# Other costs and margins in the planner that orders a hybrid attention and state-space layer on one core

## The chip, the core and the metric

The kernel runs on one core of a Trainium2 chip. A core has five engines that run at the same time, each through its own list of instructions in order: TensorE (PE, matrix products; its weight loads are shown as PEld), VectorE (DVE), ScalarE (ACT), GpSimd (POOL) and SyncE (SP), which here only issues transfers. Sixteen DMA engines carry the transfers between memory and the core's SBUF. Products land in PSUM, from where DVE and ACT take them.

The metric is the time of one execution on the device in microseconds (us). The time before is the median of three runs; beside it stands one more execution that was profiled, and everything said of single instructions comes from that one.

## The reference

One layer of a streaming encoder is computed for two groups of requests that share the weights: a prompt of 1024 tokens and eight samples of 16 tokens, 1152 tokens in all.

```
h     = rms_norm(x, norm_g) * (1 + scale) + shift          # scale, shift, gate from silu(c) @ w_ada
q, k, v, z_att, z_ssd, xbc, dt_raw, gates = split(h @ w_in)
q, k  = rms_norm per head
att   = (softmax(q k^T / 8 + bias, masked to a band of 9 chunks of 64) v * silu(z_att)) @ w_att_proj
xbc   = silu(depthwise causal conv of width 4)             # -> x, B, C of the state-space branch
y     = chunked scan with decay exp(cumsum(dt * a)) over x, B, C  + d_skip * x
ssd   = rms_norm(y * silu(z_ssd), in 4 groups) @ w_ssd_proj
out   = x + gate * ((sigmoid(g_att) * att + sigmoid(g_ssd) * ssd) @ w_out)
```

The width of the model is 1024; there are 16 attention heads of 64 and 32 state-space heads of 64 with a state of 128. The samples attend to 512 cached rows and start from given states. The last keys, values, convolution rows and states are outputs too.

## The kernel before

**Tiling.** Tokens lie along the free axis in three groups of 384. Each large product is done in f16 with the weights and the operand split into a high and a low part: high times high, high times low, low times high, three matmuls of 128x128 against 384 columns for each block of 128 of the inner dimension (lines 689, 690 and 692 in `dense`, 742 to 744 in `dense_tok`, where the tokens are the stationary side). One tile of a result takes 8 such threes. It goes into a PSUM tile of the tag "d", of which there are three places; smaller products use the tag "g" (three places) and the tag "s" (one place of two banks).

**Stages.** First the modulation and the norm (until about 80 us of the profiled span), in an order that is fixed by hand. Then eight attention units of two heads each (to about 680 us), 16 pairs of state-space heads (to about 1380 us), and the three output projections with their merge gates. Within the attention stage a unit's queries and keys are normalised on POOL (`rsqrt_small`, lines 567 to 573, a power and two Newton steps; then the scaling at line 1220), transposed on PE (line 1240, and 1256 for the samples), copied out by DVE (line 1244), multiplied into scores on PE (line 1395; 1450 and 1453 for the samples), and turned into weights by DVE and ACT. The weights are transposed by a transfer that SP issues (line 1330; line 1472 for the samples, whose result DVE then puts in order at line 1474), and PE weighs the values with them (line 1348; 1483 for the samples). In the state-space stage the transfer at line 1759 does the like.

**Weights.** SP loads raw weight blocks (line 589) into three places. ACT and DVE make the high and low parts (lines 607 and 608); ACT also takes a sum of squares of each (line 599).

**The order.** The program is first written down by generators that take turns by a rough clock. Then the class `Order` makes the order in which each engine gets its instructions. It groups instructions into units (three matmuls of a dense product, or a run of small matmuls, are one unit), numbers them as they were written, finds what each must wait for, and plays the program through with a cost for each unit: `cost` gives how long it holds its engine and when its result is there. At each step the engine that can go on first gets a unit. Among the units of that engine that can start at that time, those whose inputs have been there for a margin ("sure" ones) go first, and among these the one written first; if none is sure, the first written of those that can start:

```
can = [u for u in ready[e] if u["now"] <= t]
sure = [u for u in can if u["safe"] <= t]
u = min(sure or can, key=lambda u: u["i"])
```

The margin is `SAFE` by the waiting engine, and `SAFE_DMA` where the input comes by a transfer. Units that open a PSUM tile must also find a place of its tag free. `apply` then ties each engine to the order found. The chip does not see the costs: they only decide which instruction stands before which, and an engine whose next instruction isn't ready waits, whatever stands behind it. Instructions marked with `late` keep the order in which they were written among those of their engine; almost everything until 80 us is so marked.

The transfers are planned in eight lanes for each issuing queue, used in turn; a transfer waits until the one before it in its lane has landed.

Of the kernel before, what the change touches and what calls it, by code (L numbers as in the profile page):

```python
# [14 lines left out]
ALU = mybir.AluOpType  # L15
# [19 lines left out]
AHEAD = 2  # L35
# [27 lines left out]
SP = 2.0 ** 12  # L63
# [75 lines left out]
class Order:  # L139


    SLOTS = {"d": 3, "g": 3, "s": 1}
    SAFE = {"PE": 500.0, "DVE": 300.0, "Activation": 300.0, "Pool": 0.0, "SP": 300.0}
    SAFE_DMA = 1500.0

    def __init__(self, tc, instructions, pinned, cuts):
        self.tc = tc
        self.list = [x for x in instructions if x.opcode != "TilePoolBoundary"]
        self.pinned, self.cuts = pinned, cuts

# [38 lines left out]
    def cost(self, x):  # L189

        e, op = self.engine(x), x.opcode
        outs = [a for a in x.outs if hasattr(a, "bass_ap")]
        ins = [a for a in x.ins if hasattr(a, "bass_ap")]
        p, n, dt = self.shape(outs[0])
        m = max([n] + [self.shape(a)[1] for a in ins[:1]])
        if e == "PE":
            rows, cols = x.tile_size
            moving = self.shape(ins[0])
            rate = 0.4245 * (4 if moving[2] == "float32" else 1)
            t = max(moving[1] * rate, 52.0 if rate < 1 else 105.0) * rows * cols / 16384  # L200
            return t, t + 170
        if op == "DMACopy":
            if e == "Pool":
                return 560.0, 4500.0
            return 380.0, 2600.0 + p * n * 4 / 300.0 if n * p > 4096 else 2600.0
        if op.startswith("DmaTranspose"):
            return 1350.0 if m < 2000 else 3200.0, 3200.0 + 1.0 * m
        if e == "Activation":
            t = 205 + 0.83 * m
            return t - 100 + 93 * (len(outs) > 1), t + 95 * (len(outs) > 1)  # L210
        if e == "DVE":
            if op == "TensorCopy":
                t = 165 + 0.57 * m
            elif op == "TensorReduce":
                t = 145 + 1.05 * m
            elif op == "TensorScalarPtr" and len([a for a in ins if self.shape(a)[1] > 1]) < 2:
                t = 215 + 0.52 * m
            elif op == "Reciprocal":
                t = 240 + m
            else:  # L220
                t = (210 if dt == "float16" else 180) + 1.04 * m
            return t - 80, t + 80 * (op == "ISA")
        if op == "Memset":
            return 200.0, 210.0
        t = 200 + 1.75 * m
        return t, t + 10

    def build(self):

        units, self.of, last = [], {}, None  # L230
        for x in self.list:
            e = self.engine(x)
# [8 lines left out]
            u = {"eng": e, "ins": [x], "i": len(units), "pred": {}, "succ": [], "key": None}  # L241
# [9 lines left out]
        for x in self.list:  # L251
            u = self.of[x.name]
            e = u["eng"]
# [4 lines left out]
            for a, w in acc:  # L258
                t, name, r0, r1, c0, c1 = self.region(a)
# [23 lines left out]
        for u in units:  # L283
            costs = [self.cost(x) for x in u["ins"]]
            u["busy"] = sum(c for c, _ in costs)
            u["lat"] = u["busy"] - costs[-1][0] + costs[-1][1]
            u["dma"] = any("Dma" in x.opcode or "DMA" in x.opcode for x in u["ins"])
        self.tiles = tiles
        opener = {}
        for name, (tag, us) in tiles.items():  # L290
# [13 lines left out]
    def run(self):  # L304

        units = self.units
        left = {u["i"]: len(u["pred"]) for u in units}
        engines = ["PE", "DVE", "Activation", "Pool", "SP"]
        free = dict.fromkeys(engines, 0.0)
        ready = {e: [] for e in engines}  # L310
        start, finish = {}, {}
        slots = {t: [0.0] * n for t, n in self.SLOTS.items()}
        lanes = {"SP": [0.0] * 8, "Pool": [0.0] * 8}
        nlane = {"SP": 0, "Pool": 0}
        order = {e: [] for e in engines}
        key = [None]
        log = []

        def add(u):
            r = safe = 0.0  # L320
            for j, kind in u["pred"].items():
                v = units[j]
                if v["eng"] == u["eng"] and not v["dma"]:
                    t = finish[j] if kind == 2 and u["eng"] != "PE" else start[j]
                    m = 0.0
                else:
                    t = finish[j] + 60
                    m = self.SAFE_DMA if v["dma"] else self.SAFE[u["eng"]]
                r = max(r, t)
                safe = max(safe, t + m)  # L330
            u["r"], u["safe"] = r, safe
            ready[u["eng"]].append(u)

        for u in units:
            if not left[u["i"]]:
                add(u)
        n = 0
        while n < len(units):
            best = None
            for e in engines:  # L340
                lane = 0.0
                for u in ready[e]:
                    r = u["r"]
                    for name in u.get("opens", ()):
                        s = slots[self.tiles[name][0]]
                        need = sum(self.tiles[o][0] == self.tiles[name][0] for o in u["opens"])
                        r = max(r, sorted(s)[need - 1] if len(s) >= need else 1e18)
                    u["now"] = r
                c = [u["now"] for u in ready[e]]
                if not c or min(c) > 1e17:  # L350
                    continue
                t = max(free[e], min(c))
                if best is None or t < best[0]:
                    best = (t, e)
            assert best, ("no unit can go on", [(e, [(u["i"], u["ins"][0].name) for u in ready[e]][:4]) for e in engines])
            t, e = best
            can = [u for u in ready[e] if u["now"] <= t]
            sure = [u for u in can if u["safe"] <= t]
            u = min(sure or can, key=lambda u: u["i"])
            ready[e].remove(u)  # L360
            for name in u.get("opens", ()):
                s = slots[self.tiles[name][0]]
                s.remove(min(s))
            if u["dma"]:
                k = nlane[e] % 8
                nlane[e] += 1
                t = max(t, lanes[e][k])
                lanes[e][k] = t + u["lat"]
# [8 lines left out]
            start[u["i"]], finish[u["i"]] = t, t + u["lat"]  # L377
# [12 lines left out]
            n += 1  # L390
        self.order, self.log, self.end = order, log, max(finish.values())
        self.start, self.finish = start, finish

# [9 lines left out]
def trunk_kernel(ctx: ExitStack, tc: tile.TileContext, h, again):  # L403
    nc = tc.nc
# [82 lines left out]
    n = (HCOLS - E0 - 3 * 1184 - 1024) // 1184  # L487
# [55 lines left out]
    dma = nc.sync.dma_start  # L543

    store = nc.gpsimd.dma_start
    pinned, cuts = set(), set()
    pinning = [True]

    def late(x):
# [15 lines left out]
    def rsqrt_small(v):  # L565

        late(nc.gpsimd.memset(v[2], -0.5))
        nc.gpsimd.tensor_tensor(v[1], v[0], v[2], ALU.pow)  # L568
# [1512 lines left out]
    order = Order(tc, list(nc.cur_bb.bb.instructions), pinned, cuts)  # L2081
    order.build()
    order.run()
    order.apply()
# [1859 lines left out]
```

## Time and profile before

| what | before |
|---|---|
| median of 3 runs | 1812.56 us (1806.89 to 1813.68) |
| profiled execution | 1813.1 us |
| its span, first to last instruction | 1810.6 us |
| mean granted clock of TensorE | 0.988 |
| PE busy | 1753.5 us (97%) |
| DVE, ACT, POOL busy | 1230.5, 959.7 and 351.2 us |
| share of the transfer engines | 51.4% for SP's queue, 4.2% for POOL's |

The span is shorter than the time of the execution by 2.5 us, which lie before the first and after the last instruction that the profile shows. In the rows, "waited for" names the instruction that released the waiting one; "PEclk" is the share of its full clock that TensorE was granted; "DMA" is the mean busy share of the 16 transfer engines. A matmul's own time in a row is longer than what it adds to the stream, since the next one starts before it ends. A time beside a transfer in the chain of waits runs from its issue to its landing.

### The profile page before, as it was taken

The page shows a single profiled execution, that of the slowest core. Times are in us where ns is not written, and L with a number is a line of the kernel's source. Part 1 is how long each engine was busy: PE and PEld are TensorE (multiplying, and loading weights), DVE is VectorE, ACT ScalarE, POOL GpSimd, SP SyncE. Part 2 cuts the span into 40 slices and gives each one's busy share as a digit, 9 for nine tenths or more (in the row PEclk, how much of TensorE's full clock was granted, in tenths as well). Part 3 has the DMA queues.
Part 4 walks back from the last instruction along what each step waited for, and adds up shares of the span by engine and source line. Part 5 has one row for each costly group of instructions (what it writes and reads, how often), then busy time and mean ns, then how long its engine had stood idle before and what let it go on. Part 6 is the DMA issues. An engine that isn't in the chain of part 4 may idle for free.

```text
span 1810.6 us, 34950 instructions
## 1 busy us (share of the span) xinstructions
PE 1753.5 (97%) x13821; PEld 1104.9 (61%) x13821; DVE 1230.5 (68%) x2327; ACT 959.7 (53%) x1905; POOL 351.2 (19%) x624
## 2 busy tenths in 40 slices
PE   6999999899999999999999999999999999999998
PEld 3556556566555556666666766666666556666664
DVE  4557767777777867767777777677775436876732
ACT  6866455565565647545556556555562625332510
POOL 0124134133322201222212132213122200000000
PEclk8999999999999999999999999999999999999999
DMA  9229968979689695533454354434567734311321
GB/s 368 74 74 226 197 181 183 194 204 214 165 233 201 158 209 150 150 116 125 117 151 139 114 152 154 143 119 107 155 200 271 289 129 142 103 41 60 126 101 55
DMA packets 266565, 284.87 MB, mean 157 GB/s; under 512 B 199628, under 2 KB 200664, under 8 KB 266392
## 3 DMA queue, kind: packets, MB, share of 16 engines
q1 hardware_dynamic: 257432, 253.90, 51.4%
q0 software_dynamic: 8960, 28.65, 4.2%
q8 instruction: 110, 1.80, 0.4%
q14 instruction: 63, 0.52, 0.1%
HBM read 192.70 MB, written 43.66 MB: 131 GB/s over the span
## 4 chain that ended last, share of the span: by engine, by line
PE 80%; DMA 6%; ACT 5%; DVE 4%; POOL 3%; issue 2%; SPq 0%; DVEq 0%; ACTq 0%; POOLq 0%
PE d L689 17%; PE d L692 17%; PE d L690 17%; PE d L742 4%; PE d L744 4%; PE d L743 4%; PE g L1348 2%; DMA arena<-arena 2%; PE s L1835 2%; PE g L1807 1%; PE s L1395 1%; PE g L1855 1%; POOL arena L568 1%; PE g L1395 1%; PE g L1483 1%
## 5 line engine op out<-in xcount | busy, mean ns | idle before, releaser
L689 PE MATMUL d<-arena 128*128 128x384 f16 x2172 | 710.7, 327 | 5.3 <-DVE arena L1978 2.7
L690 PE MATMUL d<-arena 128*128 128x384 f16 x2172 | 709.7, 327 | 0.0
L692 PE MATMUL d<-arena 128*128 128x384 f16 x2172 | 709.7, 327 | 0.0
L692 PEld LDWEIGHTS <-arena 128*128 128x128 f16 x2280 | 223.3, 98 | 148.1 <-issue 1.0
L689 PEld LDWEIGHTS <-arena 128*128 128x128 f16 x2280 | 223.5, 98 | 146.9 <-issue 7.7
L690 PEld LDWEIGHTS <-arena 128*128 128x128 f16 x2280 | 223.4, 98 | 143.5 <-issue 6.7
L599 ACT ACTIVATE arena<-arena 128x1024 bf16<-128x1024 f32 (+3 forms) x169 | 181.6, 1075 | 157.1 <-DMA arena<-in_wall_dram 86.3
L608 DVE SCALAR_TENSOR_TENSOR arena<-arena 128x1024 f16<-128x1024 f32 (+1 forms) x117 | 147.7, 1264 | 77.4 <-ACT arena L607 77.0
L607 ACT ACTIVATE arena<-arena 128x1024 f16<-128x1024 f32 (+1 forms) x117 | 122.4, 1047 | 131.0 <-PE d L690 115.0
L742 PE MATMUL d<-arena 128*128 128x384 f16 (+1 forms) x568 | 187.5, 330 | 0.0
L744 PE MATMUL d<-arena 128*128 128x384 f16 (+1 forms) x568 | 187.1, 329 | 0.0
L743 PE MATMUL d<-arena 128*128 128x384 f16 (+1 forms) x568 | 187.0, 329 | 0.0
L1288 ACT ACTIVATE arena<-arena 128x640 f32<-128x640 f32 (+3 forms) x144 | 100.7, 701 | 69.3 <-DVE arena L1291 69.0
L1546 DVE SCALAR_TENSOR_TENSOR arena<-arena 128x1176 f32<-128x1176 f32 x72 | 106.3, 1476 | 6.7 <-issue 4.8
L1734 ACT ACTIVATE arena<-arena 128x128 f32<-128x128 f32 x288 | 89.6, 388 | 11.4 <-DMA arena<-acs_d 11.3
L1216 POOL TENSOR_SCALAR arena<-arena 128x16 f32<-128x16 f32 (+1 forms) x24 | 13.4, 558 | 385.0 <-DVE arena L1189 324.6
L1324 DVE SCALAR_TENSOR_TENSOR arena<-arena 128x640 f16<-128x640 f32 (+4 forms) x128 | 87.6, 720 | 0.1
L742 PEld LDWEIGHTS <-arena 128*128 128x128 f16 x576 | 56.3, 98 | 50.3 <-issue 17.4
L744 PEld LDWEIGHTS <-arena 128*128 128x128 f16 x576 | 56.5, 98 | 38.7 <-issue 0.7
L1183 ACT ACTIVATE arena<-d 128x256 f32<-128x256 f32 x71 | 26.8, 377 | 95.3 <-PE d L744 95.1
L743 PEld LDWEIGHTS <-arena 128*128 128x128 f16 x576 | 56.5, 98 | 32.5 <-issue 0.2
L568 POOL TENSOR_TENSOR arena<-arena 128x16 f32<-128x16 f32 (+2 forms) x28 | 70.2, 2507 | 2.3
(244 smaller groups left out, 2614.4 us busy)
## 6 DMA issues: line engine op xcount, KB each, us to landing
arena<-in_wall_dram SPq DMA_DIRECT2D x85, 512.0 KB, 3.9
arena<-acs_d SPq DMA_DIRECT2D x32, 576.0 KB, 5.8
arena<-in_kc_dram SPq DMA_DIRECT2D x64, 256.0 KB, 4.4
arena<-in_vc_dram SPq DMA_DIRECT2D x64, 256.0 KB, 4.0
arena<-in_wada_dram SPq DMA_DIRECT2D x24, 512.0 KB, 10.0
arena<-in_xT_dram SPq DMA_DIRECT2D x16, 576.0 KB, 5.0
arena<-eacs_d SPq DMA_DIRECT2D x32, 288.0 KB, 6.0
gate_d<-arena POOLq DMA_DIRECT2D x48, 192.0 KB, 4.4
```

Source lines behind the costliest of these rows:

```text
L599: keep(nc.scalar.activation(junk[:, :n], x, AF.Square, scale=scale * n ** -0.5, accum_out=sums[:, c:c + 1]))
L607: keep(nc.scalar.activation(hi, x, AF.Copy, scale=scale))
L608: keep(nc.vector.scalar_tensor_tensor(lo, x, scale, hi, ALU.mult, ALU.subtract))
L689: nc.tensor.matmul(ps, hi.r[:, wc], kh.r[:, tok], start=k == 0, stop=False)
L690: nc.tensor.matmul(ps, hi.r[:, wc], kl.r[:, tok], start=False, stop=False)
L692: nc.tensor.matmul(ps, lo.r[:, wc], kh.r[:, tok], start=False, stop=k == nk - 1)
L742: nc.tensor.matmul(ps, kh.r[:, tok], wh, start=k == 0, stop=False)
L743: nc.tensor.matmul(ps, kh.r[:, tok], wl, start=False, stop=False)
L744: nc.tensor.matmul(ps, kl.r[:, tok], wh, start=False, stop=k == KT - 1)
L1288: nc.scalar.activation(p, p, AF.Exp, bias=sm_[:, 4 + e:5 + e], scale=-1.0, accum_out=sm_[:, 6 + e:7 + e])
L1546: nc.vector.scalar_tensor_tensor(yc, r.ap[:, j:j + n], w4[:, i, j:j + 1], yc, ALU.mult, ALU.add)
L1734: nc.scalar.activation(me[e].ap[:, cs], me[e].ap[:, cs], AF.Relu, scale=-1.0, bias=a4[:, c, hds[e]:hds[e] + 1])
```

## The change

Only the planner's costs, margins and limits change; no instruction is added or taken away, and only the order within each engine's list can come out another way.

- **POOL's costs.** A power (line 568 only, which is entered in a new set `slow`) is costed at 250 + 180 ns for each column, where it was 200 + 1.75 ns like any other; and no POOL instruction except a memset and a transfer's issue is costed under 300 ns.
- **Transfers.** A plain transfer had a latency of 2600 ns plus its bytes at 300 a ns on SP (2600 ns if small), and 4500 ns on POOL, each on its own. Now all of both queues share one way, `bus`: a transfer gets on it 1400 ns after its issue or when the one before is through, holds it for its bytes at 360 a ns (a transposing one for 300 + 1.1 ns for each column, where its latency was 3200 + 1.0), and has landed 700 ns after that. The issue of a large transposing one is costed at 3000 ns instead of 3200.
- **Margins.** PE's goes from 500 to 1000 ns, that for transfers from 1500 to 2500 ns. A new one, `SAFE_SLOT`, makes a unit that opens a PSUM tile sure only 500 ns after the place for it is free.
- **Limit.** With `AHEAD`, no unit is taken whose number is 1200 or more above that of the first unit that isn't placed yet.

```
--- before.py
+++ after.py
@@ -140,11 +140,13 @@
 
 
     SLOTS = {"d": 3, "g": 3, "s": 1}
-    SAFE = {"PE": 500.0, "DVE": 300.0, "Activation": 300.0, "Pool": 0.0, "SP": 300.0}
-    SAFE_DMA = 1500.0
-
-    def __init__(self, tc, instructions, pinned, cuts):
-        self.tc = tc
+    SAFE = {"PE": 1000.0, "DVE": 300.0, "Activation": 300.0, "Pool": 0.0, "SP": 300.0}
+    SAFE_DMA = 2500.0
+    SAFE_SLOT = 500.0
+    AHEAD = 1200
+
+    def __init__(self, tc, instructions, pinned, cuts, slow):
+        self.tc, self.slow = tc, slow
         self.list = [x for x in instructions if x.opcode != "TilePoolBoundary"]
         self.pinned, self.cuts = pinned, cuts
 
@@ -200,11 +202,9 @@
             t = max(moving[1] * rate, 52.0 if rate < 1 else 105.0) * rows * cols / 16384
             return t, t + 170
         if op == "DMACopy":
-            if e == "Pool":
-                return 560.0, 4500.0
-            return 380.0, 2600.0 + p * n * 4 / 300.0 if n * p > 4096 else 2600.0
+            return 560.0 if e == "Pool" else 380.0, p * n * 4 / 360.0
         if op.startswith("DmaTranspose"):
-            return 1350.0 if m < 2000 else 3200.0, 3200.0 + 1.0 * m
+            return 1350.0 if m < 2000 else 3000.0, 300 + 1.1 * m
         if e == "Activation":
             t = 205 + 0.83 * m
             return t - 100 + 93 * (len(outs) > 1), t + 95 * (len(outs) > 1)
@@ -222,7 +222,8 @@
             return t - 80, t + 80 * (op == "ISA")
         if op == "Memset":
             return 200.0, 210.0
-        t = 200 + 1.75 * m
+        t = 250 + 180.0 * m if x.name in self.slow else 200 + 1.75 * m
+        t = max(t, 300.0)
         return t, t + 10
 
     def build(self):
@@ -284,7 +285,7 @@
             costs = [self.cost(x) for x in u["ins"]]
             u["busy"] = sum(c for c, _ in costs)
             u["lat"] = u["busy"] - costs[-1][0] + costs[-1][1]
-            u["dma"] = any("Dma" in x.opcode or "DMA" in x.opcode for x in u["ins"])
+            u["dma"] = u["ins"][0].opcode == "DMACopy" or u["ins"][0].opcode.startswith("DmaTranspose")
         self.tiles = tiles
         opener = {}
         for name, (tag, us) in tiles.items():
@@ -314,6 +315,7 @@
         nlane = {"SP": 0, "Pool": 0}
         order = {e: [] for e in engines}
         key = [None]
+        bus, low, done = 0.0, 0, [False] * len(units)
         log = []
 
         def add(u):
@@ -340,13 +342,14 @@
             for e in engines:
                 lane = 0.0
                 for u in ready[e]:
-                    r = u["r"]
+                    r, u["sure"] = u["r"], u["safe"]
                     for name in u.get("opens", ()):
                         s = slots[self.tiles[name][0]]
                         need = sum(self.tiles[o][0] == self.tiles[name][0] for o in u["opens"])
                         r = max(r, sorted(s)[need - 1] if len(s) >= need else 1e18)
+                        u["sure"] = max(u["sure"], r + self.SAFE_SLOT)
                     u["now"] = r
-                c = [u["now"] for u in ready[e]]
+                c = [u["now"] for u in ready[e] if u["i"] < low + self.AHEAD]
                 if not c or min(c) > 1e17:
                     continue
                 t = max(free[e], min(c))
@@ -354,18 +357,21 @@
                     best = (t, e)
             assert best, ("no unit can go on", [(e, [(u["i"], u["ins"][0].name) for u in ready[e]][:4]) for e in engines])
             t, e = best
-            can = [u for u in ready[e] if u["now"] <= t]
-            sure = [u for u in can if u["safe"] <= t]
+            can = [u for u in ready[e] if u["now"] <= t and u["i"] < low + self.AHEAD]
+            sure = [u for u in can if u["sure"] <= t]
             u = min(sure or can, key=lambda u: u["i"])
             ready[e].remove(u)
             for name in u.get("opens", ()):
                 s = slots[self.tiles[name][0]]
                 s.remove(min(s))
+            lat = u["lat"]
             if u["dma"]:
                 k = nlane[e] % 8
                 nlane[e] += 1
                 t = max(t, lanes[e][k])
-                lanes[e][k] = t + u["lat"]
+                bus = max(t + 1400, bus) + lat
+                lanes[e][k] = bus + 700
+                lat = bus + 700 - t
             busy = u["busy"]
             if e == "PE":
                 g = u["key"][1]
@@ -374,7 +380,7 @@
                 key[0] = g
             if e == "PE":
                 log.append((t, t - free[e], u))
-            start[u["i"]], finish[u["i"]] = t, t + u["lat"]
+            start[u["i"]], finish[u["i"]] = t, t + lat
             free[e] = t + busy
             order[e].append(u)
             for name in u.get("uses", ()):
@@ -388,6 +394,9 @@
                 if not left[j]:
                     add(units[j])
             n += 1
+            done[u["i"]] = True
+            while low < len(units) and done[low]:
+                low += 1
         self.order, self.log, self.end = order, log, max(finish.values())
         self.start, self.finish = start, finish
 
@@ -543,7 +552,7 @@
     dma = nc.sync.dma_start
 
     store = nc.gpsimd.dma_start
-    pinned, cuts = set(), set()
+    pinned, cuts, slow = set(), set(), set()
     pinning = [True]
 
     def late(x):
@@ -565,7 +574,7 @@
     def rsqrt_small(v):
 
         late(nc.gpsimd.memset(v[2], -0.5))
-        nc.gpsimd.tensor_tensor(v[1], v[0], v[2], ALU.pow)
+        slow.add(nc.gpsimd.tensor_tensor(v[1], v[0], v[2], ALU.pow).ins.name)
         for _ in range(2):
             nc.gpsimd.tensor_tensor(v[2], v[1], v[1], ALU.mult)
             nc.gpsimd.tensor_tensor(v[2], v[2], v[0], ALU.mult)
@@ -2078,7 +2087,7 @@
     ps = pg(1)
     nc.tensor.matmul(ps[:1], good[:, n:n + 1], ones[:, :1], start=True, stop=True)
     nc.vector.tensor_scalar(again, ps[:1], P - 0.5, None, ALU.is_lt)
-    order = Order(tc, list(nc.cur_bb.bb.instructions), pinned, cuts)
+    order = Order(tc, list(nc.cur_bb.bb.instructions), pinned, cuts, slow)
     order.build()
     order.run()
     order.apply()
```

More of the change, by code (lines that the diff above doesn't have):

```diff
@@ L142, with __init__ @@
     SLOTS = {"d": 3, "g": 3, "s": 1}
[L143 to L147, printed above, removed]
+    SAFE = {"PE": 1000.0, "DVE": 300.0, "Activation": 300.0, "Pool": 0.0, "SP": 300.0}
+    SAFE_DMA = 2500.0
+    SAFE_SLOT = 500.0
+    AHEAD = 1200
+    def __init__(self, tc, instructions, pinned, cuts, slow):
+        self.tc, self.slow = tc, slow
         self.list = [x for x in instructions if x.opcode != "TilePoolBoundary"]
@@ L202, in cost @@
         if op == "DMACopy":
-            if e == "Pool":
-                return 560.0, 4500.0
-            return 380.0, 2600.0 + p * n * 4 / 300.0 if n * p > 4096 else 2600.0
+            return 560.0 if e == "Pool" else 380.0, p * n * 4 / 360.0
         if op.startswith("DmaTranspose"):
-            return 1350.0 if m < 2000 else 3200.0, 3200.0 + 1.0 * m
+            return 1350.0 if m < 2000 else 3000.0, 300 + 1.1 * m
         if e == "Activation":
@@ L224, in cost @@
             return 200.0, 210.0
-        t = 200 + 1.75 * m
+        t = 250 + 180.0 * m if x.name in self.slow else 200 + 1.75 * m
+        t = max(t, 300.0)
         return t, t + 10
@@ L286, in build @@
             u["lat"] = u["busy"] - costs[-1][0] + costs[-1][1]
-            u["dma"] = any("Dma" in x.opcode or "DMA" in x.opcode for x in u["ins"])
+            u["dma"] = u["ins"][0].opcode == "DMACopy" or u["ins"][0].opcode.startswith("DmaTranspose")
         self.tiles = tiles
@@ L316, in run @@
         key = [None]
+        bus, low, done = 0.0, 0, [False] * len(units)
         log = []
@@ L342, in run @@
                 for u in ready[e]:
-                    r = u["r"]
+                    r, u["sure"] = u["r"], u["safe"]
                     for name in u.get("opens", ()):
@@ L347, in run @@
                         r = max(r, sorted(s)[need - 1] if len(s) >= need else 1e18)
+                        u["sure"] = max(u["sure"], r + self.SAFE_SLOT)
                     u["now"] = r
-                c = [u["now"] for u in ready[e]]
+                c = [u["now"] for u in ready[e] if u["i"] < low + self.AHEAD]
                 if not c or min(c) > 1e17:
@@ L356, in run @@
             t, e = best
-            can = [u for u in ready[e] if u["now"] <= t]
-            sure = [u for u in can if u["safe"] <= t]
+            can = [u for u in ready[e] if u["now"] <= t and u["i"] < low + self.AHEAD]
+            sure = [u for u in can if u["sure"] <= t]
             u = min(sure or can, key=lambda u: u["i"])
@@ L363, in run @@
                 s.remove(min(s))
+            lat = u["lat"]
             if u["dma"]:
@@ L367, in run @@
                 t = max(t, lanes[e][k])
-                lanes[e][k] = t + u["lat"]
+                bus = max(t + 1400, bus) + lat
+                lanes[e][k] = bus + 700
+                lat = bus + 700 - t
             busy = u["busy"]
@@ L376, in run @@
                 log.append((t, t - free[e], u))
-            start[u["i"]], finish[u["i"]] = t, t + u["lat"]
+            start[u["i"]], finish[u["i"]] = t, t + lat
             free[e] = t + busy
@@ L390, in run @@
             n += 1
+            done[u["i"]] = True
+            while low < len(units) and done[low]:
+                low += 1
         self.order, self.log, self.end = order, log, max(finish.values())
@@ L545, in trunk_kernel @@
     store = nc.gpsimd.dma_start
-    pinned, cuts = set(), set()
+    pinned, cuts, slow = set(), set(), set()
     pinning = [True]
@@ L567, in rsqrt_small @@
         late(nc.gpsimd.memset(v[2], -0.5))
-        nc.gpsimd.tensor_tensor(v[1], v[0], v[2], ALU.pow)
+        slow.add(nc.gpsimd.tensor_tensor(v[1], v[0], v[2], ALU.pow).ins.name)
         for _ in range(2):
@@ L2080, in trunk_kernel @@
     nc.vector.tensor_scalar(again, ps[:1], P - 0.5, None, ALU.is_lt)
-    order = Order(tc, list(nc.cur_bb.bb.instructions), pinned, cuts)
+    order = Order(tc, list(nc.cur_bb.bb.instructions), pinned, cuts, slow)
     order.build()
```

## The prediction

> **What bounds the kernel now.** I read the head of the page first, then the busy times by stage, then PE's waits.
>
> ```profile
> span 1810.6 us, 34950 instructions
> ...
> 0.00:80.00 80.00, 61.49 (x395) 36.05 (x396) 46.07 (x68) 63.11 (x108) 0.84 (x8) 0.91 0.67 250
> 80.00:680.00 600.00, 575.43 (x5568) 348.42 (x5567) 432.47 (x1125) 341.89 (x821) 178.95 (x313) 0.98 0.78 184
> 680.00:1380.00 700.00, 697.38 (x5237) 468.04 (x5236) 509.37 (x768) 404.80 (x772) 156.98 (x280) 1.00 0.48 142
> 1380.00:1476.00 96.00, 93.31 (x625) 56.15 (x622) 46.26 (x58) 40.28 (x60) 14.39 (x24) 0.98 0.69 251
> 1476.00:1811.00 335.00, 325.93 (x2008) 196.22 (x2006) 196.37 (x310) 109.63 (x146) 0.00 (x0) 0.99 0.28 91
> ```
>
> The columns are the stretch, its length, busy PE, PEld, DVE, ACT and POOL, PEclk, DMA share and GB/s. PE is the bound in every stage; the next engine, DVE, is busy 432 of 600 and 509 of 700 us. An order can only win back time in which PE stands still or runs at a low clock. The idle 18.5 us of the first stage lie in the order fixed by hand, and the 9.1 us of the last hold the end of the program; I leave both. What is open is 24.6 + 2.6 + 2.7 = 29.9 us in the three stages between. PE's waits name nearly all of it:
>
> ```profile
> PE g L1240 <- POOL arena L1220: 8.2, 4, 3.2
> ...
> PE g L1483 <- DVE arena L1474: 5.1, 2, 4.2
> PE g L1395 <- DVE arena L1403: 3.5, 1, 3.5
> PE g L1665 <- DVE arena L1501: 3.1, 1, 3.1
> PE d L689 <- DVE arena L1978: 2.7, 1, 2.7
> PE g L1483 <- DVE arena L1244: 2.5, 1, 2.5
> ...
> PE d L689 <- DVE arena L1705: 1.6, 1, 1.6
> ...
> PE g L1348 <- DMA arena<-arena: 1.3, 2, 0.9
> PE d L689 <- ACT arena L1527: 1.1, 1, 1.1
> ```
>
> Each row is who waited for whom, us in all, times and the longest. They sum to 29.1 us. The stalls have a second price, seen in PE's instructions around the first:
>
> ```profile
> 87.41 0.33 PE L744 MATMUL d<-arena 128*128 128x384 f16 x1
> 90.52 1.12 PE L1240 MATMUL g<-arena 128*128 128x128 f32 x4 [2.78 <-POOL arena L1220]
> 91.42 0.53 PE L742 MATMUL d<-arena 128*128 128x384 f16 x1
> ```
>
> After 2.78 us of idleness the same product takes 0.53 instead of 0.33 us. Seven such places, in the columns of the stage view:
>
> ```profile
> 86.00:96.00 10.00, 7.22 (x37) 4.56 (x36) 2.17 (x4) 2.31 (x6) 3.73 (x10) 0.83 0.01 2
> 176.00:192.00 16.00, 11.69 (x156) 7.01 (x154) 10.40 (x38) 8.02 (x24) 0.90 (x4) 0.89 0.75 189
> 318.00:332.00 14.00, 9.46 (x143) 6.20 (x139) 8.01 (x26) 8.03 (x24) 0.00 (x0) 0.88 0.97 236
> 524.00:536.00 12.00, 9.49 (x141) 5.66 (x140) 8.98 (x25) 10.90 (x27) 0.34 (x1) 0.86 0.97 313
> 586.00:598.00 12.00, 8.30 (x124) 6.06 (x123) 7.85 (x14) 7.32 (x19) 9.80 (x23) 0.86 0.40 121
> 660.00:682.00 22.00, 17.59 (x183) 12.13 (x182) 9.63 (x12) 12.44 (x24) 1.76 (x6) 0.92 0.73 183
> 1440.00:1452.00 12.00, 9.31 (x51) 5.46 (x49) 5.36 (x6) 3.01 (x5) 0.00 (x0) 0.86 0.76 305
> ```
>
> Length times the missing share of the clock is 1.7 us in each (10 x 0.17, 16 x 0.11, and so on), 11.9 us in all. So no order of these instructions can win more than about 29.1 + 11.9 = 41 us: 1772 us is the floor.
>
> [...]
>
> **POOL's costs.** What the old planner missed is in POOL's rows:
>
> ```profile
> L568 POOL TENSOR_TENSOR arena<-arena 128x16 f32<-128x16 f32 x16 | 50.0, 3125 | 1.3
> ...
> L1220 POOL TENSOR_TENSOR arena<-arena x24: 612/1901/2815, 88.6 to 596.8; 128x1024 f32<-128x1024 f32 x16, 128x256 f32<-128x256 f32 x8
> ```
>
> The power on 16 columns was costed at 200 + 28 = 228 ns and takes 3125: the plan had the scaled q and k 2.9 us too early, and PE's margin was 0.5. That leaves a wait of up to 2.4 us from this alone, and the other eight steps of the chain at 228 ns too add to it; the waits at line 1240 reach 3.2 us. The new cost is 250 + 16 x 180 = 3130 ns. So PE's turn for line 1240 moves back behind work that is there: in the rows above, line 742's products follow the stall directly, and they could have stood before it. Removed: 8.2 us of waits, and the clock of the places at 86 and 586, 3.4 us: 11.6 us. What is late next are ACT and DVE on lines 1241 and 1244, by nothing, since the chain itself ends when it did.
>
> [...]
>
> **Transfers.** Three more groups of waits go back to transfers that came later than planned, in rows of the chain of waits (start, time from issue to landing). Below them stands what SP issued up to the second of them, from its instructions in order of time:
>
> ```profile
> 178.30 5.18 DMA arena<-arena
> ...
> 315.66 8.76 DMA arena<-arena
> ...
> 1434.54 8.87 DMA arena<-gate_d
> ```
>
> ```profile
> 308.89 2.08 SPq L1467 DMA_DIRECT2D arena<-in_vc_dram  x4
> 311.07 0.38 SPq L1199 DMA_DIRECT2D out_v_dram<-arena  x1
> 311.54 0.38 SPq L589 DMA_DIRECT2D arena<-in_wall_dram  x1
> 312.02 2.28 SPq L1330 DMA_TRANSPOSE arena<-arena  x1
> 314.39 1.07 SPq L589 DMA_DIRECT2D arena<-in_wall_dram  x2
> 315.66 2.76 SPq L1472 DMA_TRANSPOSE arena<-arena  x1
> ```
>
> The transposing transfer of 315.66 lands after 8.76 us. The old plan gave it 3.2 + 1.28 = 4.5 us, plus 1.5 of margin: DVE stood at line 1474 before its data were there, and PE at line 1483 for 4.2 us. By the new rule and the sizes of the tiles in the code (128 rows of 512, 640 and 1024 words) the bus takes 4 x 0.73 us for the four at line 1467, 0.91 for line 1199, 1.46 for each of three at line 589 and at most 1.71 for the transposing one, 9.9 in all from 308.89 + 1.4: free at 320.2. The late one lands at 320.2 + 1.7 + 0.7 = 322.6 and is sure at 325.1; in fact it landed at 324.4. For this one the new rule is right where the old was 4.3 us off. Where nothing is in the way the new allowance is 1.4 + 1.7 + 0.7 + 2.5 = 6.3 us, which holds the 5.18 us of 178.30 too. I charge to transfers: lines 1474 (5.1), 1403 (3.5; DVE stood behind the transfer of 178.30), 1348 (1.3) and 1978 (2.7; the transfer of 1434.54), 12.6 us, and the clock at 176, 318 and 1440, 5.1: 17.7 us. I take three quarters, 13.3, since a consumer that finds no sure work beside it is still placed early; the ends are nothing (the waits move to other transfers) and 17.7.
>
> **Waits for DVE and ACT.** Lines 1501, 1244, 1705 and 1527 (3.1 + 2.5 + 1.6 + 1.1 = 8.3 us) with the clock at 524 and 660 (3.4) make 11.7 us. DVE's and ACT's own costs do not change; what changes is that they stand less behind late transfers, and PE's margin of 1.0 us in place of 0.5. I take half, 5.9; the ends are nothing and 11.7.
>
> **The margins' own price.** With a longer margin PE prefers later work and the attention chain is served later: by at most 0.5 us at each product, and 1.0 more behind a transfer. As long as dense products are there this costs nothing on PE; without that cover it costs idle time. A new order also makes new waits. I count two, at the size of line 1483's mean and line 1978's (2.6 and 2.7 us) with 1.7 us of clock each: 8.7 us; the ends are none and, from today's seven, about 31 us (7 x 2.7 + 11.9). The margin for PSUM places costs a dense tile nothing: its place is one of three, and a tile of 24 matmuls, 0.16 us apart, takes 3.9 us.
>
> **The limit.** The units are some 8,000 (2880 threes of dense products, and DVE's, ACT's, POOL's and SP's instructions), so 1200 of them are about 270 of 1811 us, nearly four attention units of 75 us. Buffers hold fewer. I cost it at nothing; bounds are nothing and the slow rival below, whose cover it would take away.
>
> **Sum.** 11.6 + 13.3 + 5.9 - 8.7 = 22.1 us off 1813.1, the profiled execution's own time (span 1810.6 and 2.5 around it): 1791.0. That execution lies 0.5 us above the median of 1812.56, so I predict 1790.5 us.
>
> **The rivals.**
>
> *Waits are exchanged, not removed.* POOL's part is won, but a new order of the same length meets other late transfers. Then 11.6 us won stand against two or three more new waits of 4.4 us: 1805 to 1814, say 1808. For it speaks that today's stalls came out of many free choices, so some are chance; against it that the new rule gets the worst transfer right.
>
> *The longer margins use up the cover.* With PE's margin doubled and a transfer's 1 us longer, a unit's six rounds of scores and weights each start up to 2 us later, 12 us in a unit. PE fills this with the next unit's projections: 288 threes, 47 us of the 75. It decides if these run out before the last round is weighed. Then each of the eight units ends in a stall like the worst seen, 4.2 + 1.7 us, 47 us; with POOL's 11.6 won the time is 1848. Half of it would be 1825. Against it: behind the first stall stood line 742's products, so cover was left there; for it: nothing in the rows shows how much.
>
> *The plan hardly changes where it matters.* If most units have only one candidate at their turn, margins choose nothing, and only POOL's costs act: 1801.
>
> **How the numbers follow.** A measurement here tells about 0.5% (9 us) from no change. The forecast (1774 to 1803) gets 0.58; only POOL's costs acting, 1801, 0.08; waits exchanged, 0.19; cover used up, wholly or in part, 0.15. Faster by over 0.5% (below 1803.5) takes the first two and little of the third, 0.66; the rest of the third is the same, 0.18; slower 0.16. The range of 8 in 10 goes from 1774, near the floor, to 1816, which leaves out the cover case and little else.
>
> **What would show it.** Right: line 1240 no longer waits for line 1220; lines 1474 and 1403 vanish from PE's waits; PE's idle time between 80 and 1476 us falls from 29.9 to under 15 us; its clock there is 1.00 but for two or three places. POOL's and DVE's busy times stay. Wrong: as many stalls under other names; idle PE at the end of attention units with no dense product behind it; stages that end later at the same busy time of PE, which would mean that a changed order costs PE more than its waits.

## The result and the profile after

The kernel after takes 1782.11 us (median of 6 runs, 1778.59 to 1783.71), the one before 1813.12 us in the same comparison (6 runs). The ratio is 0.9831, with a 95% interval of 0.9813 to 0.9849: faster by 1.7%. The profiled execution took 1782.14 us at a span of 1780.1 us, against 1813.1 and 1810.6. The forecast was 1790.5 us: the way and the range were right, the size was 8 us short.

The stages of the kernel after, at the same times of the span as before (stretch, length, busy PE, PEld, DVE, ACT, POOL, granted clock, share of the transfer engines, GB/s):

```profile
0.00:80.00 80.00, 67.02 (x460) 38.44 (x461) 48.25 (x72) 64.99 (x120) 8.29 (x20) 1.00 0.67 250
80.00:680.00 600.00, 589.76 (x5703) 355.44 (x5702) 452.72 (x1141) 362.65 (x860) 174.82 (x308) 1.00 0.79 191
680.00:1380.00 700.00, 695.08 (x5241) 467.66 (x5240) 507.87 (x766) 386.17 (x727) 161.29 (x283) 1.00 0.50 150
1380.00:1476.00 96.00, 96.00 (x607) 56.43 (x606) 38.17 (x51) 37.68 (x56) 6.72 (x13) 1.00 0.51 179
1476.00:1811.00 335.00, 295.19 (x1819) 177.74 (x1817) 187.72 (x298) 106.14 (x142) 0.00 (x0) 0.99 0.26 83
```

Between 80 and 1476 us PE is idle for 10.2 + 4.9 + 0.0 = 15.1 us, where it was 29.9, and its clock there rounds to 1.00. The first 80 us have changed too: 13 us idle instead of 18.5, and a clock of 1.00 instead of 0.91. All of this is read at the same times of the span; the kernel after is ahead there, so the stretches do not hold quite the same work. PE's waits after (line numbers are 9 higher than before):

```profile
PE g L819 <- DMA arena<-in_xT_dram: 8.1, 1, 8.1
PE g L1492 <- DVE arena L1483: 3.2, 1, 3.2
PE d L698 <- DVE arena L1714: 2.7, 1, 2.7
PE g L1249 <- POOL arena L1229: 2.3, 2, 1.3
PE g L1889 <- POOL rarena L1805: 2.0, 1, 2.0
PE g L1265 <- ACT arena L1498: 1.6, 1, 1.6
...
PE g L1404 <- DVE arena L1300: 0.9, 1, 0.9
PE g L1357 <- DMA arena<-arena: 0.8, 2, 0.5
```

The wait for POOL at the scaling has gone from 8.2 to 2.3 us (line 1240 before, 1249 after). The waits at lines 1395 for 1403, 1665 for 1501 and 689 for 1978 are gone. The one at line 1483 for 1474 (now 1492 for 1483) is still there with 3.2 us, and line 1889 is new. The one at line 698 for 1714 stood before too (689 for 1705), with 1.6 us.

Where the time went, stage by stage, is read from the first and last start of products that mark them (ns of one, then first and last start in us). First the kernel before, then the kernel after: the end of the fixed start, the beginning and the end of the state-space stage, and the last product.

```profile
L898 PE MATMUL s<-arena x48: 322/326/528, 35.1 to 69.7; 128*128 128x384 f16 x48
L1665 PE MATMUL g<-arena x36: 272/273/299, 672.4 to 1209.2; 128*128 128x128 f32 x36
L1835 PE MATMUL s<-arena x512: 272/273/324, 712.2 to 1380.5; 128*64 128x128 f32 x171
L2079 PE MATMUL g<-arena x2: 163/164/164, 1803.0 to 1803.0; 128*1 128x1 f32 x2
```

```profile
L907 PE MATMUL s<-arena x48: 322/326/336, 23.4 to 58.4; 128*128 128x384 f16 x48
L1674 PE MATMUL g<-arena x36: 272/273/329, 645.4 to 1183.0; 128*128 128x128 f32 x36
L1844 PE MATMUL s<-arena x512: 272/273/323, 680.4 to 1354.3; 128*64 128x128 f32 x171
L2088 PE MATMUL g<-arena x2: 163/164/164, 1772.3 to 1772.3; 128*1 128x1 f32 x2
```

The start became 11.3 us shorter (69.7 to 58.4), the attention stage 15.7 (602.7 to 587.0), the projections 4.5 (422.5 to 418.0); the state-space stage is 0.8 longer. The 11.3 us were not in the prediction. ScalarE's and PE's instructions in order of time show what they are, first before, then after:

```profile
9.31 1.28 ACT L1587 ACT_TABLE_LOAD   x1
16.58 0.23 ACT L1587 ACTIVATE arena<-arena 128x32 f32<-128x32 f32 x1 [5.99 <-DMA arena<-in_par_dram]
16.71 2.20 ACT L805 ACTIVATE arena<-arena 128x1152 f32<-128x1152 f32 x2
...
24.35 4.08 PE L812 MATMUL g<-arena 128*128 128x48 f32 x18 [7.06 <-DVE arena L806]
```

```profile
9.59 1.16 ACT L814 ACTIVATE arena<-arena 128x1152 f32<-128x1152 f32 x1 [0.31 <-DMA arena<-in_xT_dram]
...
17.30 2.15 PE L821 MATMUL g<-arena 128*128 128x48 f32 x18
```

Line 1587 is the exponential of the state-space branch's decay rates. Its result is first used, after a change of sign, some 600 us later (line 1589, at 613.7 us), but its only input is the block of parameters. So the old planner could put it into the fixed start: that transfer of 125 KB was issued at 6.68 us, and by the old cost it lands 2.6 + 0.4 us after its issue. It landed after 9.9, at 16.6: ScalarE stood for 5.99 us, the squares of the norm (line 805) stood behind it, DVE's sums behind those and behind the change of sign (line 1588), for which DVE stood 6.1 us. PE stood 7.06 us in front of the column sums. The kernel after takes the exponential at 386.0 us.

### The profile page after: what moved, and what is told of

It reads as the page before. It is cut to its first block, busy times and chain, and to the rows that moved or that the text cites. A ratio compares the mean times of both kernels' runs of the same rounds, so it can differ in the third digit from the quotient of the medians.

```text
span 1780.1 us, 34953 instructions
## 1 busy us (share of the span) xinstructions
PE 1743.0 (98%) x13821; PEld 1095.7 (62%) x13821; DVE 1234.7 (69%) x2327; ACT 957.6 (54%) x1903; POOL 351.1 (20%) x624
## 4 chain that ended last, share of the span: by engine, by line
PE 81%; ACT 7%; DMA 5%; DVE 3%; POOL 2%; issue 1%; SPq 0%; DVEq 0%; ACTq 0%; POOLq 0%
PE d L698 17%; PE d L699 17%; PE d L701 17%; PE d L751 5%; PE d L753 4%; PE d L752 4%; PE g L1357 2%; PE s L1844 1%; PE g L1816 1%; ACT arena L1743 1%; DMA arena<-arena 1%; PE g L1864 1%; PE s L1404 1%; DMA arena<-in_wall_dram 1%; PE g L1404 1%
## 5 line engine op out<-in xcount | busy, mean ns | idle before, releaser
L1297 ACT ACTIVATE arena<-arena 128x640 f32<-128x640 f32 (+4 forms) x144 | 100.7, 701 | 66.1 <-DVE arena L1300 65.9
L1225 POOL TENSOR_SCALAR arena<-arena 128x16 f32<-128x16 f32 (+1 forms) x24 | 11.2, 468 | 366.4 <-DVE arena L1198 331.4
L1749 DVE TENSOR_TENSOR arena<-arena 128x1152 f32<-128x1152 f32 x32 | 45.9, 1434 | 39.2 <-ACT arena L1747 39.2
```

Source lines behind the costliest of these rows:

```text
L1297: nc.scalar.activation(p, p, AF.Exp, bias=sm_[:, 4 + e:5 + e], scale=-1.0, accum_out=sm_[:, 6 + e:7 + e])
```

## The experiments

Each is timed beside the kernel before on the same chip, in one of several comparisons, so ratios and not times are to be set against each other. The ratio is the comparison's own estimate with its 95% interval; it differs by up to 0.001 from the quotient of the two medians. The table gives each one's stages as read above, as differences from the kernel before (us of one profiled execution), and the time with its ratio.

The stages of a row are those of one execution, which can lie some us off the median: POOL's costs alone 5.9 us below it, the transfers' margin alone 3.8 below, POOL's costs and transfers 4.2 above. And a product that is placed on the other side of a mark moves time from one column to the next.

| kernel | start | attention | state space | projections | time | ratio |
|---|---|---|---|---|---|---|
| after | -11.3 | -15.7 | +0.8 | -4.5 | 1782.11 | 0.9831 (0.9813 to 0.9849) |
| limit alone | -11.2 | -2.7 | 0.0 | +1.4 | 1802.28 | 0.9950 (0.9931 to 0.9970) |
| exponential held back | -11.3 | -0.2 | -1.1 | +2.5 | 1802.51 | 0.9950 (0.9928 to 0.9972) |
| after, no limit | -11.4 | -18.1 | +0.4 | -4.5 | 1779.05 | 0.9822 (0.9801 to 0.9843) |
| POOL's costs alone | -1.1 | -8.8 | -5.6 | -2.4 | 1801.16 | 0.9942 (0.9923 to 0.9961) |
| transfers, rule and margin | -10.9 | -3.4 | -2.9 | -4.5 | 1790.88 | 0.9864 (0.9840 to 0.9888) |
| transfers' rule alone | -10.5 | -14.6 | +2.3 | -4.5 | 1785.63 | 0.9843 (0.9827 to 0.9860) |
| transfers' margin alone | -1.6 | +0.3 | -4.5 | -0.9 | 1809.84 | 0.9976 (0.9960 to 0.9993) |
| PE's and PSUM margins alone | -1.3 | -1.5 | -5.7 | +1.5 | 1805.10 | 0.9942 (0.9923 to 0.9961) |
| POOL's costs and transfers | -11.3 | -14.6 | +2.0 | -4.5 | 1781.01 | 0.9809 (0.9785 to 0.9833) |
| after, margins doubled | -9.3 | -15.7 | -6.1 | -4.5 | 1777.15 | 0.9789 (0.9762 to 0.9816) |
| after, margins times four | -10.5 | +24.3 | -11.9 | -4.4 | 1809.52 | 0.9976 (0.9964 to 0.9988) |
| doubled, POOL's wide ones dearer | -9.1 | -16.3 | -5.6 | -4.5 | 1777.56 | 0.9796 (0.9779 to 0.9814) |

**The limit alone, in the kernel before.**

```
+    AHEAD = 1200
...
-                c = [u["now"] for u in ready[e]]
+                c = [u["now"] for u in ready[e] if u["i"] < low + self.AHEAD]
...
-            can = [u for u in ready[e] if u["now"] <= t]
+            can = [u for u in ready[e] if u["now"] <= t and u["i"] < low + self.AHEAD]
```

> The kernel before with the limit of 1200 units alone; costs and margins stay. Theory (the limit keeps the exponential of the decay rates, line 1587 before, out of the fixed start, where ScalarE waited 6 us for its parameters and PE then 7 us): the start ends about 11 us earlier, and the time falls by 9 to 13 us, to about 1802. Rival (the start got faster by the transfers' new rule, the limit binds nowhere, as I predicted): within 4 us of 1813.

Measured: 1802.28 against 1810.86 us, 8.6 us less, a little under the 9 to 13 expected, and the start 11.2 us shorter. The limit, which I had costed at nothing, is worth half a per cent in the old planner.

**Only the exponential held back, in the kernel before.** The limit applies to two instructions, the exponential and the change of sign (the test in the planner is left out here):

```
-        late(nc.scalar.activation(nega, par["a_log"], AF.Exp))
-        nc.vector.tensor_scalar(nega, nega, -1.0, None, ALU.mult)
+        x_ = nc.scalar.activation(nega, par["a_log"], AF.Exp)
+        held.add(late(x_).ins.name)
+        held.add(nc.vector.tensor_scalar(nega, nega, -1.0, None, ALU.mult).ins.name)
```

> The kernel before, with the same limit on two instructions only: the exponential at line 1587 and the sign change behind it. Theory (this one instruction is what the limit is worth): as with the whole limit, within 3 us of it, about 1802. Rival (the limit is worth something for other units too): clearly nearer to 1813 than with the whole limit.

Measured: 1802.51 us, the same as with the whole limit. PE's start in it:

```profile
15.25 1.98 PE L815 MATMUL g<-arena 128*128 128x512 f32 x4 [0.31 <-DMA arena<-in_xT_dram]
17.23 2.21 PE L817 MATMUL g<-arena 128*128 128x48 f32 x18
```

The 7 us of idleness in front of the column sums are gone, as in the kernel after. One instruction of 0.23 us, in a place 380 us earlier than it has here (399.6), had cost 11 us of the start. What the limit does beside that cannot be told from nothing.

**The kernel after without the limit.**

```
-    AHEAD = 1200
+    AHEAD = 1000000
```

> The kernel after with the limit put out of reach; all else stays. Theory: the exponential goes back to the start, but behind the squares, because the shared way lets the parameters land later in the plan; it costs two table loads of 1.3 us there, so 1784 to 1788. Rival (the limit carries the whole gain of the start): 11 us slower, about 1793.

Measured: ratio 0.9822 against 0.9831 for the kernel after; the intervals overlap for the most part, and the start is as short (-11.4). The exponential does come back into the start, at 17.87 us, but behind the squares, as it does with the transfers' rule alone (17.9). By the new rule the eight loads of x issued from 1.17 us on (128 x 1152 words, 1.64 us each) hold the way until about 15.7 us, so the parameters come later in the plan than the old cost had them. So the limit is a second guard against what the transfers' rule already prevents. The 2 to 6 us that I expected for the two table loads do not show.

**POOL's costs alone, in the kernel before.** The edit is the change's own: the set `slow`, 250 + 180 ns a column, and the floor of 300 ns.

> The kernel before with the new costs of POOL alone. Theory as predicted: PE no longer waits at line 1240 for line 1220 (8.2 us), with the clock 11.6 us, so about 1801. Rival (waits are exchanged): within 5 us of 1813, with as much idle time of PE under other names. The start stays slow in both.

Measured: 1801.16 against 1810.86 us, 9.7 us less. The row of its PE's waits:

```profile
PE g L1241 <- POOL arena L1221: 3.3, 3, 1.5
```

From 8.2 to 3.3 us, no stall over 1.5, and the start nearly as slow as before: as predicted in place and, at 11.6 predicted, in size.

**The transfers' rule and margin, in the kernel before**, and then each alone. The new costs of a transfer go with the rule, and so does the change's narrower test of which units are transfers; both are left out here.

```
+    SAFE_DMA = 2500.0
...
+                bus = max(t + 1400, bus) + lat
+                lanes[e][k] = bus + 700
+                lat = bus + 700 - t
```

> The kernel before with the transfers' new rule and their margin of 2500 ns alone. Theory (the rule repairs the start by itself, since it lands the parameters later in the plan, and three quarters of the stalls behind transfers go): 9 us from the start and about 13 us from the stalls, so 1786 to 1792. Rival (the rule only repairs the start, since a consumer with no sure work beside it is placed early as before): about 1802, with PE's waits at lines 1483 and 1395 (lines of before) still there.

> The kernel before with the transfers' new rule on the old margin of 1500 ns. Theory (the rule does the start by itself, 11 us, and most of the rest): 1791 to 1799. Rival (without the longer margin the rule only repairs the start, or not even that, since a free way lets a transfer land earlier than the old cost): 1801 or more.

> The kernel before with the transfers' margin of 2500 instead of 1500 ns alone, on the old costs. Theory (the rule of one shared way did the work): the start stays slow, and at most 6 us come off, 1807 to 1813. Rival (the margin did it): 1795 or less.

Measured: 1790.88 against 1814.46 us with both; 1785.63 against 1812.79 with the rule; 1809.84 against 1812.79 with the margin. The rule does the work, 27 us, of which 10.5 in the start; that is more than the 1791 to 1799 expected. The longer margin adds nothing to it that can be measured (the profiled attention stage is even 11 us longer with both). Of the waits that the rival of the first run named, the old line 1395's for 1403 is gone in both, line 1483's for 1474 is left with 3.3 us (rule) and 3.6 (both). Both with the rule still have the wait for POOL; the row is that of the rule alone:

```profile
PE g L1242 <- POOL arena L1222: 8.3, 4, 3.2
```

So the rule alone comes as low as the whole change, as far as the intervals tell: 0.9827 to 0.9860 against 0.9813 to 0.9849, with PE still standing 8.3 us for POOL.

**PE's margin and that for PSUM places, in the kernel before.**

```
-    SAFE = {"PE": 500.0, ...
+    SAFE = {"PE": 1000.0, ...
+    SAFE_SLOT = 500.0
...
+                        u["sure"] = max(u["sure"], r + self.SAFE_SLOT)
```

> The kernel before with PE's margin of 1000 ns and the one for PSUM places of 500 ns alone. Theory (a margin of 1.0 us is less than POOL's error of 3.5 us and than most late transfers, so it takes 0.5 us off each stall): 2 to 5 us faster, about 1807. Rival (margins use up the cover): slower than before by over 5 us.

Measured: 1805.10 against 1814.46 us, more than the 2 to 5 us expected. Of the profiled execution's 7.0 us, 5.7 lie in the state-space stage. Its waits show most of it: before, PE waited there 3.1 us at line 1665 for 1501, and the granted clock of the stage's first 100 us was 0.98; with these margins that wait is gone and the clock there is 1.00, some 3.1 + 1.7 us. The transfers' margin alone, which takes 4.5 us off that stage, has lost it too, and POOL's costs alone has 1.8 us of it left. The kernel after has lost it as well, but has the waits at line 698 for 1714 and 1889 for 1805 (2.7 + 2.0 us, each with loss of clock) instead, so its stage is 0.8 us longer: in this stage waits were exchanged. Why three unlike edits remove or shorten the same wait is open.

**POOL's costs and transfers together, without limit, PE's and PSUM margins.**

> The kernel before with POOL's new costs and the transfers' new rule and margin, without the limit and without PE's and the PSUM margins. Theory (these two carry nearly the whole change): 1778 to 1786. Rival (PE's margin is what turns right costs into fewer stalls): 1790 or more.

Measured: 1781.01 against 1814.46 us, ratio 0.9809, the whole change within its interval. These two carry it. Its wait for POOL is down from the rule's 8.3 us:

```profile
PE g L1243 <- POOL arena L1223: 3.0, 3, 1.5
```

Yet its profiled attention stage is as long as with the rule alone (588.1 us both), and the intervals of the two overlap. Beside the rule with the longer margin, in the same comparison, POOL's costs take 9.9 us (1790.88 to 1781.01). So what they are worth beside the rule lies somewhere between nothing and 10 us. The four parts alone take 8.6, 9.7, 23.6 and 9.4 us off, 51 in all, and together 31: the limit and the transfers' rule win the same 11 us of the start, and the other parts overlap too: the margins, which win 9.4 us alone, show no gain once the costs are right.

**All three margins doubled, then four times as long, in the kernel after.**

```
-    SAFE = {"PE": 1000.0, ...       SAFE_DMA = 2500.0       SAFE_SLOT = 500.0
+    SAFE = {"PE": 2000.0, ...       SAFE_DMA = 5000.0       SAFE_SLOT = 1000.0
+    SAFE = {"PE": 4000.0, ...       SAFE_DMA = 10000.0      SAFE_SLOT = 2000.0
```

> The kernel after with all three margins doubled (2000, 5000 and 500 to 1000 ns). Theory (cover is plentiful, the stalls left are 2 to 3 us long): 1777 to 1783, fewer stalls, no new idle time at the ends of units. Rival (longer margins use up the cover, as my slow case had it): slower than the kernel after by over 5 us, 1788 or more, with PE waiting at the ends of the attention units.

> The kernel after with its three margins four times as long (4000, 10000 and 2000 ns). Theory (cover is plentiful: the next unit's and the next pair's products are always there): within 4 us of the doubled margins, 1774 to 1781. Rival (my slow case: the longer margins use up the cover, only later than thought): 1790 or more, the loss in the attention stage, with PE waiting there.

Measured: doubled, 1777.15 us, ratio 0.9789, the fastest of all, though its interval touches that of the kernel after. Four times, 1809.52 against 1812.79 us: some 32 us slower than with doubled margins. My theory of plentiful cover fell between the two. The attention stage is 24.3 us longer than even before. PE's waits with fourfold margins:

```profile
PE s L1459 <- DMA arena<-in_kc_dram: 6.3, 6, 1.2
PE g L1492 <- DVE arena L1483: 5.8, 2, 3.1
PE d L751 <- ACT arena L1193: 3.9, 4, 2.1
PE g L1404 <- DVE arena L1300: 1.9, 4, 0.9
```

The first of these rows does not exist in the kernel after: PE stands six times at the samples' scores for keys that have not landed. Between the fixed start and the state-space stage PE is idle for 24.2 us (10.9 in the kernel after), at a clock of 0.98 (1.00), and 28 more matmuls lie before that mark (5633 against 5605), which move some of the state-space stage's time into this one. My reading is that with margins that long dense products are pulled forward and used up; then nothing is sure, and the planner falls back on the first written unit that can start by the plan, with no margin at all. The runs do not show this, since what was sure at each step was not recorded. The time and the stage are those of this run's rival; the prediction's slow case (1825 to 1848) is not reached. And the waits rise at several places rather than once at each unit's end, so neither that case's mechanism nor the end of units as its place is shown.

**Doubled margins and POOL's wide instructions costed higher.**

```
-        t = 250 + 180.0 * m if x.name in self.slow else 200 + 1.75 * m
+        t = 250 + 180.0 * m if x.name in self.slow else (420 if m > 64 else 200) + 1.75 * m
```

> The kernel after with its three margins doubled, and POOL's instructions of more than 64 columns costed 220 ns higher (868 for 256 columns, where the profile has 849 and the planner 648). Theory (of the stalls that the doubled margins leave, the longest is at line 1889 behind POOL's line 1805, 2.4 us with its clock): 3 to 5 us below the doubled margins, 1772 to 1775. Rival (a changed cost only exchanges waits): 1775 to 1782.

Measured: ratio 0.9796 against 0.9789, no difference. The wait that it was to remove is even longer, here with doubled margins and then with the higher cost too:

```profile
PE g L1889 <- POOL rarena L1805: 3.3, 2, 2.4
```

```profile
PE g L1889 <- POOL rarena L1805: 4.1, 2, 2.6
```

220 ns were not its cause. In the kernel after, the chain in front of it (start, us, instruction) shows ScalarE's row of short instructions, then a gate's tanh, then its store on POOL's queue, and only then line 1805:

```profile
697.91 2.63 ACT arena L1743 x9
...
701.63 0.48 ACT arena L1647
...
702.40 0.54 POOL gate_d L1648
...
702.96 0.64 POOL rarena L1805
...
703.64 1.36 PE g L1889 x4
```

POOL stood for 4.70 us at a store that waited for ScalarE. That the plan had ScalarE earlier is a guess, and whether a better cost for ScalarE removes the wait was not tried.

## Why the prediction was right and where it was not

**What bounds the kernel.** Right: PE's idle time and clock were what could be won. The floor of 1772 us was too high by what I left out. I set the first stage aside because its order is fixed by hand, and quoted its row with 18.5 us idle and a clock of 0.91 (80 x 0.09 = 7 us) without asking what was in it. The order of the marked instructions is fixed against each other, but an unmarked one could still be put between them, and one was. This step failed, and it is the whole difference: of the 30.7 us up to the last product, 11.3 came from the start and 19.4 from the stages that I had summed up to 22.1.

**POOL's costs.** Predicted 11.6 us, alone 9.7 measured. The mechanism held: the power on 16 columns, which took 3125 ns before and 3089 after on average, is costed at 3130 ns instead of 228, and the stalls at the scaling shrank to at most 1.5 us. A remainder of 3.3 us of waits alone, and 2.3 in the kernel after, is left of the 8.2 that the forecast took off whole. The scaling, line 1229 in the kernel after, takes 1902 ns at the median there and up to 2735, where the planner has 1992 for its wide form; what lengthens the longest, and whether the remainder comes from that, no run shows. What the runs took away is the independence of this term: with the transfers' rule in place and the stalls for POOL still there (8.3 us), the kernel was already as fast as the whole change, within the intervals.

**Transfers, and waits for DVE and ACT.** Predicted 13.3 + 5.9 us. The rule alone gave 16.8 us outside the start (-14.6 + 2.3 - 4.5), so the size was right. My worked example was not. In it the rule lands the transfer at 322.6 us and it landed at 324.4, so only the margin covered it. In the kernel after, the same transfer (the sixth of the sixteen at the old line 1472) landed as late as before, and PE stood at line 1492 for 3.2 us. The chain of waits of the kernel after:

```profile
296.23 8.56 DMA arena<-arena
...
304.88 0.89 DVE arena L1483
...
306.02 1.30 PE g L1492 x40
```

With the same transfers in front of it, and one transposing one more, the rule gives a landing about 302.8, sure at 305.3, and it was 304.8. I had compared the rule's margin with the landing and not asked whether the planner had anything sure to put before it; it may place a unit unsure. Whether it did so here is open, since the planner's own times were not recorded. The waits at the old lines 1403 and 1978 went, as predicted, with the projections' 4.5 us.

**The margins' price.** Two new waits were put at 8.7 us with the clock. Two places lost clock in the kernel after, at line 698 for 1714 (2.7 us) and line 1889 for 1805 (2.0 us); with 2 x 1.7 us of clock this is 8.1 us. The size agrees, but the margins are not what it is the price of. The kernel with the transfers' rule alone, on the old margins, has the same two waits:

```profile
PE d L691 <- DVE arena L1707: 3.6, 2, 2.7
...
PE g L1882 <- POOL rarena L1798: 2.0, 1, 2.0
```

They belong to the new order, which the prediction gave as the second half of this term. PE's and the PSUM margins by themselves won 9.4 us in the old planner. In the new one, margins of up to twice the change's length cost nothing that can be measured; at four times they do.

**The sum.** Part of its nearness is luck. POOL's costs alone (9.7 us) and the rule alone outside the start (16.8) make 26.5 us, and all together gave 19.4 there. The missing 7 us are near the 8.7 that I had charged to the margins, but no run shows the margins costing them: I read them as overlap of the parts.

**The limit.** Costed at nothing, with nothing as the bound on the side of a gain: wrong alone (8.6 us), right beside the transfers' rule, as far as the intervals tell. I looked only at whether it could starve PE, not at what it would keep from being placed too early.

**The rivals.** Exchange of waits was true in part: those that are left stand at other places, but there are fewer. "Only POOL's costs act" fell, since the rule alone is worth more. The slow case did not come at these margins; at four times the gain is gone (1809.52 us), short of that case's 1825 to 1848 and with its mechanism not shown. Two numbers in the rivals' working were off, without bearing on the forecast: "288 threes, 47 us" are 288 matmuls, at 0.163 us each, and two or three new waits of 4.4 us against 11.6 won give about 1810 to 1814, not 1805 to 1814.

**The signs.** Half of them came. The wait at line 1395 for 1403 vanished, the clock is 1.00 but for two places, and POOL's and DVE's busy times stayed (351.1 and 1234.7 us, from 351.2 and 1230.5). The waits for line 1220 and at line 1483 for 1474 shrank but stayed, and PE's idle time came to 15.1 us, just over the 15.

## What to carry to other kernels

When a planner sets the order, read what stands in front of every stall on its engine, in the fixed parts too: an instruction with a distant use and an early input can be placed anywhere, and where it waits for a transfer everything behind it waits (here ScalarE for 5.99 us and PE, behind it, for 7.06). Correct the costs that are wrong by microseconds first; here the rule of one shared way for the transfers was enough, by itself, for a gain (27 us) that cannot be told from the whole. Margins then mattered little up to twice their length, and at four times they cost more than they ever won. Parts of such a change are not worth their sum, and a wait that is long in the profile need not be worth its length beside another repair: try the parts alone and together.

## What the hardware showed beside

In these traces the length of a stall alone did not decide whether PE's clock fell with it. Three stalls of the kernel after (3.2, 2.0 and 2.7 us), in the view by stretches:

```profile
300.00:310.00 10.00, 6.77 (x85) 3.97 (x83) 6.47 (x27) 5.54 (x20) 0.00 (x0) 1.00 0.99 212
699.00:709.00 10.00, 8.03 (x40) 4.53 (x38) 8.70 (x9) 5.02 (x12) 3.48 (x6) 0.83 0.21 73
1069.00:1079.00 10.00, 7.29 (x40) 4.83 (x38) 8.57 (x8) 6.32 (x10) 0.86 (x2) 0.84 0.54 162
```

The wait of 3.2 us near 303 us left the clock at 1.00; those of 2.0 us near 702 and of 2.7 us near 1073 took 1.7 and 1.6 us of it. In the kernel before each of the seven places with 2.5 us or more in the middle stages had lost it (a clock of 0.83 to 0.92 in the stretches around them). So 1.7 us a stall was a fair price for most of these stalls, and one of the ten did not pay it. What decides it is not shown.
